# A two-block network on one core: the first block's projections multiply the raw input, and the tokens' norm factors follow on the products

## The chip, the core and the metric

The kernel runs on one core of one Trainium2 chip, in one launch. The metric is the device time of an execution in microseconds (us), lower is better. Before the change three executions took 1520.32, 1525.59 and 1520.54 us, with a median of 1520.54. The profile comes from a further execution.

## What is computed

256 tokens of width 1024 pass through two network blocks. The first block starts with an RMS norm and one wide projection of the normalised tokens, whose columns feed a recurrent mixer (RWKV), a sparse attention (its queries, keys, values and an index of keys) and two gates:

```
def rmsnorm(x, g):
    xf = x.astype(jnp.float32)
    y = xf * lax.rsqrt(jnp.mean(xf * xf, axis=-1, keepdims=True) + NORM_EPS)
    return (y * g.astype(jnp.float32)).astype(x.dtype)
...
        u = rmsnorm(h, norm1_g)
        proj = u @ w_in
...
        p_rwkv, p_att, p_idx, p_gate = jnp.split(proj, c, axis=-1)
        y_a = rwkv7_mix(token_shift(p_rwkv, tshift_mu), ...)
...
        q, k, v = rope(hv(q)), rope(hv(k)), hv(v)
...
        y_b = dsa_attention(q, k, v, q_idx, k_idx, w_idx)
        g_a, g_b = jnp.split(jax.nn.sigmoid(p_gate), 2, axis=-1)
        merged = g_a * (y_a @ w_o_rwkv) + g_b * (y_b @ w_o_att)
```

A feed-forward layer ends the first block. The second block (a gated delta rule, a dilated attention, then 64 routed experts) takes the larger part of the time and isn't touched by the change.

The norm multiplies all 1024 features of a token by one number, the token's factor rs = 1 / sqrt(mean of squares + eps). A factor per token may stand before the projection or behind it: (rs · x · g) @ w = rs · ((x · g) @ w).

## The kernel before

**Layout.** Activations lie transposed: features on the 128 partitions, tokens along a row. The input `xT` (in the trace `hT`) is 8 feature blocks of 128 x 256. A projection is cut into groups of 256 output columns. The weights of one group are one load of 1 MB (`w`, line 258, issued by SyncE), into two buffers in turn.

**Exact products from short ones.** Each fp32 operand is split in two parts of a shorter float type: a high part (`wh`, a cast on ScalarE, line 272) and the rest (`wl`, a subtraction on VectorE, line 273), in pieces of 128 x 512. The input is split likewise into `uh` and `ul`. `mm3` makes three products of one block: uh·wh, ul·wh, uh·wl. `dense` (line 300) does this for 8 feature blocks and 2 halves of the columns: 48 products of 128 x 256 into one PSUM tile `dps`. All matmuls are recorded at line 286, transposes at 289, so tiles tell them apart.

**The head of the program.** `Rms.pair` (line 373) squares the input (`nsq`, ScalarE), VectorE adds the two blocks of a pair, and TensorE multiplies by a column of ones, which gives the sum of squares of every token (`nps`). `columns` takes the root on ScalarE (line 394) and the reciprocal on VectorE (line 395): `rsc`, one factor per token on the partitions. `rows` spreads it by another product into `rsp`, where the factors lie along a row. `scaled_parts` (line 420) then computes u = x · gain · rs on VectorE (line 426), block by block, and splits it (lines 428 and 429). A `hold` keeps the first weight casts behind the root on ScalarE.

**What follows.** Seven `shift_group` calls (line 459) make the columns of the recurrent mixer: first group 6 (`lor0`), then r, k and v of two halves `g`. Each reads `dps` on ScalarE (line 465) and VectorE (line 466). `rwkv(g)` (line 547) is a long chain over small products. Of its steps these matter here: the VectorE product at line 623 ends `aa`; GpSimd scales it to `bp` and `kp` (lines 628 and 629); TensorE transposes v, `bp` and `kp` (`tps`); and products `mps` follow. `dsa_proj` makes the columns of the attention; `rope` turns them with tables `cos` and `sin`. `gate_steps` makes the gates `ga` and `gb`, four groups each. In `select` VectorE finds the best 64 keys per token (lines 832 to 836), and `attend` makes the softmax `lx`, which TensorE transposes into `xps`.

**What sets the order.** The program is written in the order of the data. A scheduler at build time puts the instructions of all engines into fixed queues by its own estimate of when each can start, so products of later groups fill TensorE between the steps of the chains. On the chip each engine works through its queue in that order.

Of the kernel before, what the change touches and what calls it, by code (L numbers as in the profile page):

```python
# [9 lines left out]
F32 = mybir.dt.float32  # L10
F32R = mybir.dt.float32r
AF = mybir.ActivationFunctionType
ALU = mybir.AluOpType
# [180 lines left out]
def _body(es, tc, A, pat, cat, taps, upto):  # L194
# [45 lines left out]
    more = [None, 0, 0, ""]  # L240
    npart = [0]

    hold = []

    def more_slots(pool_, n, tag="wm"):

        more[:] = [pool_, n, 0, tag]
# [13 lines left out]
    def wsplit(w):  # L261

        out = []
        for o in range(0, w.shape[-1], 1024):
            x = w[:, o:min(o + 1024, w.shape[-1])]
            n = x.shape[-1]
            npart[0] += 1
            hi, lo = (wp.tile([128, 1024], F32R, name="w" + q, tag="w%s%d" % (q, npart[0] % 3), bufs=1) for q in "hl")
            for c in range(0, n, 512):
                e = min(n, c + 512)  # L270
                with tc.issue_after(hold[0]) if hold else nullcontext():
                    nc.scalar.copy(hi[:, c:e], x[:, c:e])  # L272
# [91 lines left out]
    class Rms:  # L364


        def __init__(self, h, ring, gain=None):
            self.h, self.ring, self.gain = h, ring, gain
            self.p = pt("d", "nps")

            nc.scalar.activation(nrm, epsd[:, 0:1], AF.Sqrt)

        def pair(self, g):
            sq = self.ring("nsq")
            nc.scalar.activation(sq, self.h[:, 2 * g:2 * g + 2], AF.Square)
            if self.gain is not None:
                sg = self.ring("nsg")[:, 0, :]
                c = [self.gain[:, 2 * g + b:2 * g + b + 1] for b in range(2)]
                nc.vector.tensor_scalar(sg, sq[:, 0, :], c[0], None, op0=ALU.mult)
                nc.vector.scalar_tensor_tensor(sg, sq[:, 1, :], c[1], sg, op0=ALU.mult, op1=ALU.add)  # L380
                self.sums(2, sg, g)
            nc.vector.tensor_tensor(sq[:, 0, :], sq[:, 0, :], sq[:, 1, :], op=ALU.add)
            self.sums(0, sq[:, 0, :], g)

        def sums(self, o, x, g):

# [30 lines left out]
    def parts():  # L417
        return tuple(ap_.tile([128, NB, S], F32R, name="u" + x, tag="u" + x, bufs=1) for x in "hl")

    def scaled_parts(h, gain, rs, sh=None):  # L420

        hi, lo = parts()
        t = ap_.tile([128, NB, S], F32, name="u", tag="s1", bufs=1)
        for b in range(NB):
            x, xh, xl = t[:, b, :], hi[:, b, :], lo[:, b, :]
            nc.vector.scalar_tensor_tensor(x, h[:, b, :], gain(b), rs, op0=ALU.mult, op1=ALU.mult)
            if sh is None:
                nc.scalar.copy(xh, x)
# [12 lines left out]
    hc = lambda h: slice(64 * h, 64 * (h + 1))  # L441
    r2 = lambda g: lambda name: rp.tile([128, 2, S], F32, name=name, tag="r2%d" % g, bufs=NR2)

    norm = Rms(xT, r2(0))
    for g in range(4):
        norm.pair(g)
    _, uu, _ = scaled_parts(xT, lambda b: pcol("norm1_g", b), norm.rows(norm.columns()))
    hold.append(norm.root.ins)


    omm = rp.tile([128, 14], F32, name="omm")
# [6 lines left out]

    def shift_group(g, dst):
        p = yield from dense(A["w_in"][g], uu)  # L460
        for i in range(2):
            j = 2 * g + i
            q = p[:, 256 * i:256 * (i + 1)]
            d = dst[:, i, :]
            nc.scalar.activation(d, q, AF.Copy, scale=omm[:, j:j + 1])
            nc.vector.scalar_tensor_tensor(d[:, 1:], q[:, 0:S - 1], pcol("tshift_mu", j), d[:, 1:],
                                           op0=ALU.mult, op1=ALU.add)
# [53 lines left out]
                    nc.scalar.copy(part(XT, 1 - side), part(p.rearrange("p (u x) -> p u x", x=128), 1 - side))  # L521

    lor0 = r2(0)("lor0")
    whole(shift_group(6, lor0))
    hold.clear()
    lor = rp.tile([128, 2, S], F32, name="lor")
    sgd = rp.tile([128, S], F32, name="sgd")
    nc.gpsimd.memset(lor[64:128, 0, :], 0.0)
# [242 lines left out]
    def dsa_proj():  # L771

        p = yield from dense(A["w_ix"], uu, m=72)
        xi, xj = d2("xi"), d2("xj")
        nc.gpsimd.memset(xi[64:128, 0, :], 0.0)
        nc.scalar.copy(xi[0:72, 0, :], p[0:72, 0:S])
        for a in range(2):
            nc.sync.dma_start(out=xj[32 * a:32 * a + 32, 0, :], in_=xi[32 * (a ^ 1):32 * (a ^ 1) + 32, 0, :])
        for n in range(2):
            p = pt("d", "wps")  # L780
            mm(p[:, 0:8], xi[:, 0, 128 * n:128 * (n + 1)], cc("widx"), start=True, stop=True)
            nc.scalar.activation(wi[:, n, :], p[:, 0:8], AF.Copy, scale=float(64 ** -0.5 * 8 ** -0.5))
        nc.vector.tensor_tensor(xi[0:64, 1, :], xi[0:64, 0, :], cc("cos", 64), op=ALU.mult)
        nc.vector.tensor_tensor(xj[0:64, 1, :], xj[0:64, 0, :], cc("sin", 64), op=ALU.mult)
        nc.vector.tensor_tensor(ki[0:64, 0, :], xi[0:64, 1, :], xj[0:64, 1, :], op=ALU.add)
        nc.sync.dma_start(out=ki[64:128, 1, :], in_=ki[0:64, 0, :])
        for i in range(2):
            rope((yield from dense(A["w_in"][13 + i], uu)), [(every, qi[:, 2 * i:2 * i + 2])])
        for i in range(2):
            rope((yield from dense(A["w_in"][7 + i], uu)), [(every, qT[:, 2 * i:2 * i + 2])])  # L790
        for i in range(2):
            rope((yield from dense(A["w_in"][9 + i], uu)), [(hf, kz[hf, 2 * i:2 * i + 2, a, :]) for a, hf in enumerate(halves)])
        for i in range(2):
            p = pt("d", "vps")
            for k, (wh, wl) in enumerate(wblocks(A["w_in"][11 + i], 256)):
                for n in range(2):
                    tk = slice(128 * n, 128 * (n + 1))
                    mm3(p[:, 256 * n:256 * (n + 1)], (uu[0][:, k, tk], uu[1][:, k, tk]), (wh, wl), k == 0 and n == 0, k == NB - 1)
                yield
            nc.scalar.copy(vt[:, :, 256 * i:256 * (i + 1)], p.rearrange("p (n c) -> p n c", n=2))  # L800

    ga = ap_.tile([128, NB, S], F32, name="ga", tag="s1", bufs=1)
    gcol = lambda t, g: fl(t[:, 2 * g:2 * g + 2])

    def gate_steps(t, src):

        nc.scalar.activation(t, (yield from dense(src, uu)), AF.Tanh, scale=0.5)

    for g in range(2):
        whole(rkv_proj(g))  # L810
        whole(rwkv(g, yA[:, 2 * g:2 * g + 2]))
    whole(dsa_proj())
    for g in range(4):
        fill.add("ga", gate_steps(gcol(ga, g), A["w_in"][15 + g]))


    bias = dp.tile([128, 2, S], F32, name="bias")
# [84 lines left out]
    for g in range(4):  # L902
        first_term(gcol(ga, g), A["wo_r"][g], ysp, 4)
    for g in range(4):
        gate_group(gcol(gb, g), g, A["w_in"][19 + g])
    tap("ya", fl(yA))
    tap("yb", fl(yB))
    if upto == 2:
# [942 lines left out]
```

## Time and profile before

| | |
|---|---|
| median of three executions | 1520.54 us (1520.32 to 1525.59) |
| the profiled execution | 1519.02 us |
| its span, first to last instruction | 1517.2 us |
| TensorE busy with matmuls | 1439.3 us, 95% of the span |
| VectorE, ScalarE, GpSimd busy | 54%, 39%, 8% |
| HBM read | 357.51 MB, 236 GB/s over the span |

Times in the trace count from the span's start. A row of the timeline gives start, duration, engine, line, operation, output <- inputs with shapes, how many instructions were merged, and in brackets the engine's idle time before it with what ended that. PE is TensorE, PEld its weight load, DVE is VectorE, ACT ScalarE, POOL GpSimd and SP SyncE. The matmuls overlap in their pipeline, so what one costs is the distance from its start to the next one's start, not its duration. [...]

### The profile page before, as it was taken

What the parts mean: (1) busy time and instruction counts of PE and PEld (TensorE: products, weight loads), DVE (VectorE), ACT (ScalarE), POOL (GpSimd) and SP (SyncE); (2) the same over time, 40 slices, a digit from 0 to 9 for tenths busy, and PEclk for the clock granted to TensorE, in tenths of its full rate; (3) what the DMA queues carried; (4) which work ended last, traced back from release to release, by engine and by line L of the source; (5) the groups of instructions that cost most, each with busy time, mean ns of one, the idle gap of its engine ahead of it and who ended that gap; (6) DMA issues with size and microseconds to landing.
All of it is one profiled execution on the core that took longest, in us unless ns stands there. A gap on an engine that the chain in (4) does not pass through costs nothing. (4 is left out here: it accounts for less than half of the span.)

```text
span 1517.2 us, 28014 instructions
## 1 busy us (share of the span) xinstructions
PE 1439.3 (95%) x11310; PEld 1155.6 (76%) x11310; DVE 816.5 (54%) x1673; ACT 588.2 (39%) x1208; POOL 119.5 (8%) x120
## 2 busy tenths in 40 slices
PE   6999999989999979899999999999999999988997
PEld 6788998989999969798898999997554544543543
DVE  4787498568888867845854677653122111211211
ACT  5543256545444457434624555552111111111110
POOL 2143210000000000310230000100000000000000
PEclk9999999989999989899999999999999999999999
DMA  5311144649977345221321433875999999999996
GB/s 197 125 47 44 65 160 140 222 144 423 402 292 294 114 151 189 84 84 60 136 84 56 168 111 112 335 286 198 355 407 422 422 422 422 421 422 422 421 423 263
DMA packets 58627, 362.10 MB, mean 239 GB/s; under 512 B 6912, under 2 KB 7552, under 8 KB 20352
## 3 DMA queue, kind: packets, MB, share of 16 engines
q1 hardware_dynamic: 56912, 357.77, 60.6%
q10 hardware_dynamic: 1584, 2.52, 0.5%
q8 instruction: 90, 1.47, 0.4%
q14 instruction: 41, 0.34, 0.1%
HBM read 357.51 MB, written 1.05 MB: 236 GB/s over the span
## 5 line engine op out<-in xcount | busy, mean ns | idle before, releaser
L286 PE MATMUL dps<-uh,wh 128*128 128x256 f32 x1280 | 375.9, 294 | 4.1 <-ACT wh L272 2.1
L286 PE MATMUL dps<-uh,wl 128*128 128x256 f32 x1280 | 364.9, 285 | 4.0 <-DVE wl L273 4.0
L286 PE MATMUL dps<-ul,wh 128*128 128x256 f32 x1280 | 365.6, 286 | 0.1
L286 PEld LDWEIGHTS dps<-uh,wh 128*128 128x128 f32 x1280 | 244.7, 191 | 14.8 <-issue 8.6
L286 PEld LDWEIGHTS dps<-uh,wl 128*128 128x128 f32 x1280 | 244.3, 191 | 6.3 <-DVE wl L273 4.8
L286 PEld LDWEIGHTS dps<-ul,wh 128*128 128x128 f32 x1280 | 244.4, 191 | 5.8 <-issue 4.3
L273 DVE TENSOR_TENSOR wl<-w,wh 128x512 fp32r<-128x512 f32 x267 | 192.3, 743 | 59.4 <-ACT wh L272 58.0
L286 PE MATMUL gup<-wx,xg 128*32 128x512 f32 (+2 forms) x1016 | 205.0, 615 | 17.7 <-DMA wx<-in_w_exp_dram 17.6
L272 ACT CAST wh<-w 128x512 fp32r<-128x512 f32 x267 | 154.3, 615 | 143.0 <-PE dps L286 97.2
L272 ACT CAST wh<-wm 128x512 fp32r<-128x512 f32 x200 | 116.2, 618 | 128.8 <-PE dps L286 84.3
L286 PEld LDWEIGHTS gup<-wx,xg 128*32 128x32 f32 (+2 forms) x1016 | 58.5, 123 | 140.9 <-issue 106.8
L273 DVE TENSOR_TENSOR wl<-wm,wh 128x512 fp32r<-128x512 f32 x200 | 138.2, 721 | 50.6 <-ACT wh L272 48.8
L1695 DVE TENSOR_TENSOR yl<-dnp,yh 128x512 fp32r<-128x512 f32 x54 | 37.3, 691 | 154.5 <-ACT yh L1694 154.5
L1669 DVE COPY cs<-pxt 128x1 f32<-128x1 f32 x27 | 4.3, 158 | 215.2 <-PE pxt L289 215.2
L286 PE MATMUL dnp<-wx,hT 128*32 128x512 f32 (+1 forms) x528 | 101.5, 597 | 2.4 <-DMA wx<-in_w_exp_dram 1.7
L1675 ACT ACTIVATE sgx<-gup 128x256 f32<-128x256 f32 x27 | 10.4, 385 | 221.3 <-PE gup L286 221.3
L1694 ACT CAST yh<-dnp 128x512 fp32r<-128x512 f32 x54 | 31.7, 587 | 120.6 <-PE dnp L286 120.6
L286 PEld LDWEIGHTS dnp<-wx,hT 128*32 128x32 f32 (+1 forms) x528 | 28.0, 120 | 49.5 <-issue 41.3
L286 PE MATMUL acc<-PT,yh 128*128 128x256 f32 x216 | 55.1, 293 | 0.0
L286 PE MATMUL gat<-P,hth 128*128 128x256 f32 (+1 forms) x224 | 54.7, 287 | 0.0
L286 PE MATMUL acc<-PT,yl 128*128 128x256 f32 x216 | 53.0, 283 | 0.6 <-DVE yl L1695 0.6
L971 DVE SCALAR_TENSOR_TENSOR ada<-wm,ct,ada 128x512 f32<-128x512 f32 x76 | 53.2, 745 | 0.0
(530 smaller groups left out, 2786.9 us busy)
## 6 DMA issues: line engine op xcount, KB each, us to landing
wx<-in_w_exp_dram SPq DMA_DIRECT2D x159, 1024.0 KB, 16.0
w<-in_w_in_dram SPq DMA_DIRECT2D x44, 1024.0 KB, 4.9
wm<-in_w_ada_dram SPq DMA_DIRECT2D x22, 1024.0 KB, 8.6
wm<-in_w_in_dram SPq DMA_DIRECT2D x21, 1024.0 KB, 4.9
wh<-in_w_exp_dram SPq DMA_DIRECT2D x33, 512.0 KB, 15.9
wl<-in_w_exp_dram SPq DMA_DIRECT2D x33, 512.0 KB, 14.7
wm<-in_ffn_in_dram SPq DMA_DIRECT2D x16, 1024.0 KB, 10.4
wm<-in_ffn_out_dram SPq DMA_DIRECT2D x7, 1024.0 KB, 10.0
```

The source lines that it names most:

```text
L272: nc.scalar.copy(hi[:, c:e], x[:, c:e])
L273: nc.vector.tensor_sub(lo[:, c:e], x[:, c:e], hi[:, c:e].bitcast(F32))
L286: latest[0] = nc.tensor.matmul(*args, **kw)
L971: nc.vector.scalar_tensor_tensor(y, x, ct[:, k:k + 1], y, op0=ALU.mult, op1=ALU.add)
L1669: nc.vector.tensor_copy(self.cs, px[:, 256:257])
L1675: nc.scalar.activation(sg, self.pg[:, 0:256], AF.Silu)
L1694: nc.scalar.copy(yh[:, quar(c, 512)], pd)
L1695: nc.vector.tensor_tensor(yl[:, quar(c, 512)], pd, yh[:, quar(c, 512)].bitcast(F32), op=ALU.subtract)
```

## The change

The input is split right after it has landed: `raw_pair` casts x · gain on ScalarE and takes the rest on VectorE, without rs. The squares are still made first, but their sums (`finish`), the root, the reciprocal and the spreading come once the first group's 48 products have been written (`factors`). From there the factors are put in behind: `times_rs` multiplies a PSUM tile of 128 x 512 in place on VectorE, for 7 groups of the mixer, 4 of `ga` and 4 of `gb`, 15 in all. For queries and keys the factor goes into the `cos` and `sin` tables once, on GpSimd. For the attention's values and the index weights it is a per-partition scale of ScalarE's copy out of PSUM. The `hold` on the first weight casts is gone.

```
@@ Rms @@
-            self.sums(0, sq[:, 0, :], g)
+            if self.later is None:
+                self.sums(0, sq[:, 0, :], g)
+            else:
+                self.later.append((sq[:, 0, :], g))
+
+        def finish(self):
+            self.p = pt("d", "nps")
+            for x, g in self.later:
+                self.sums(0, x, g)
...
+    def raw_pair(u, h, gain, g):
+        hi, lo = u
+        for b in (2 * g, 2 * g + 1):
+            nc.scalar.activation(hi[:, b, :], h[:, b, :], AF.Copy, scale=gain(b))
+            nc.vector.scalar_tensor_tensor(lo[:, b, :], h[:, b, :], gain(b), hi[:, b, :].bitcast(F32), op0=ALU.mult, op1=ALU.subtract)
...
-    norm = Rms(xT, r2(0))
+    norm = Rms(xT, r2(0), None, [])
+    uu = parts()
     for g in range(4):
         norm.pair(g)
-    _, uu, _ = scaled_parts(xT, lambda b: pcol("norm1_g", b), norm.rows(norm.columns()))
-    hold.append(norm.root.ins)
...
+    def factors():
+        norm.finish()
+        rsc.append(norm.columns())
+        nc.vector.tensor_scalar(rsw, rsc[0], float(64 ** -0.5 * 8 ** -0.5), None, op0=ALU.mult)
+        nc.scalar.copy(rsr, norm.rows(rsc[0]))
+
+    def times_rs(p):
+        p3 = p.rearrange("p (a s) -> p a s", a=2)
+        nc.vector.tensor_tensor(p3, p3, rsr.unsqueeze(1).to_broadcast([128, 2, S]), op=ALU.mult)
+        return p
...
     def shift_group(g, dst):
         p = yield from dense(A["w_in"][g], uu)
+        if not rsc:
+            factors()
+        times_rs(p)
...
-    whole(shift_group(6, lor0))
-    hold.clear()
+    steps = shift_group(6, lor0)
+    for g in range(4):
+        raw_pair(uu, xT, lambda b: pcol("norm1_g", b), g)
+        for _ in range(2 if g else 0):
+            next(steps)
+    whole(steps)
...
                 load_consts(rp, 1)
+                for t in ("cos", "sin"):
+                    nc.gpsimd.tensor_tensor(cc(t), cc(t), rsr, op=ALU.mult)
...
-            nc.scalar.copy(vt[:, :, 256 * i:256 * (i + 1)], p.rearrange("p (n c) -> p n c", n=2))
+            for n in range(2):
+                nc.scalar.activation(vt[:, n, 256 * i:256 * (i + 1)], p[:, 256 * n:256 * (n + 1)], AF.Copy, scale=rsc[0][:, n:n + 1])
...
-    def gate_steps(t, src):
-        nc.scalar.activation(t, (yield from dense(src, uu)), AF.Tanh, scale=0.5)
+    def gate_steps(t, src, first=False):
+        p = yield from dense(src, uu)
+        nc.scalar.activation(t, times_rs(p) if first else p, AF.Tanh, scale=0.5)
```

The scheduler orders the queues anew, which the diff doesn't show. Three places follow, each row an instruction in its queue's order. Line numbers of the changed kernel are its own (283 is its matmul, 286 its transpose, 270 its `wl`, 476 its `times_rs`).

**The head, on TensorE**, before:

```order
L286 MATMUL nps<-ones,nsq 128x1 x8
L286 MATMUL rsp<-cst_74,rsc 128x128 x2
L286 MATMUL dps<-uh,wh 128x256
L286 MATMUL dps<-ul,wh 128x256
L286 MATMUL dps<-uh,wh 128x256
```

and now, where the fifth row is the third of the group's 48 products, the row of "..." stands for the rest of them, and the last row opens the second group:

```order
L283 MATMUL dps<-uh,wh 128x256
L283 MATMUL dps<-ul,wh 128x256
L283 MATMUL nps<-ones,nsq 128x1 x5
L283 MATMUL dps<-uh,wl 128x256
...
L283 MATMUL nps<-ones,nsq 128x1 x3
L283 MATMUL rsp<-cst_74,rsc 128x128 x2
L283 MATMUL dps<-uh,wh 128x256
```

Five of the eight sums stand behind the first two products, three behind the 48th, and the second group waits behind the spreading `rsp`.

**The same head on ScalarE**, now, from the squares to the first reads of the group's result:

```order
L374 ACTIVATE nsq<-hT 128x512 x4
L486 DMA low_107<-in_lowrank_dram 128x512
L486 DMA low_108<-in_lowrank_dram 128x512
L431 ACTIVATE uh<-hT,par 128x256 x4
L269 CAST wh<-w 128x512 x4
L431 ACTIVATE uh<-hT,par 128x256 x4
...
L269 CAST wh<-w 128x512
L401 ACTIVATE rsc<-nps,epsd 128x2
L269 CAST wh<-w 128x512
L471 COPY rsr<-rsp 128x256
L497 ACTIVATE lor_111<-dps,omm 128x256 x2
```

The root (`rsc`), once ahead of every weight cast, now stands behind the first cast of the third group's weights, and both `low` loads are issued ahead of the first `uh`.

**Inside the first `rwkv` chain, on TensorE**, before (`bp` and `kp` are GpSimd's outputs, 30 products of `dps` stand where the row of "..." is):

```order
L286 MATMUL bps<-rk,cst_74 128x256 x2
L289 MATMUL tps<-cst_74,v 128x128 x2
L286 MATMUL dps<-uh,wl 128x256
...
L289 MATMUL tps<-cst_74,bp 128x128
L289 MATMUL tps<-cst_74,kp 128x128
L286 MATMUL dps<-ul,wh 128x256
```

and now:

```order
L283 MATMUL bps<-rk,cst_74 128x256 x2
L286 MATMUL tps<-cst_74,v 128x128 x2
L286 MATMUL tps<-cst_74,bp 128x128
L286 MATMUL tps<-cst_74,kp 128x128
L283 MATMUL dps<-uh,wl 128x256
L286 MATMUL tps<-cst_74,bp 128x128
L283 MATMUL dps<-uh,wh 128x256
L286 MATMUL tps<-cst_74,kp 128x128
L283 MATMUL dps<-ul,wh 128x256
```

The transposes of `bp` and `kp` have moved ahead of those 30 products, which now follow the `mps` products. On VectorE one `wl` that stood between the two products of `aa` went behind them, and a `times_rs` came in ahead of them.

**In `select`, on VectorE**, the queue ahead of the first `lx` that TensorE transposes, before:

```order
L851 TENSOR_SCALAR st<-st 128x2
L273 TENSOR_TENSOR wl<-w,wh 128x512
L835 MAX m_2446<-sc 128x8
L273 TENSOR_TENSOR wl<-w,wh 128x512
L836 MATCH_REPLACE sc<-m_2446,sc 128x256
L854 RECIPROCAL st<-st 128x2
L273 TENSOR_TENSOR wl<-w,wh 128x512
L835 MAX m_2449<-sc 128x8
L855 TENSOR_TENSOR lx<-lx,st 128x2x128
```

and now:

```order
L892 TENSOR_SCALAR st<-st 128x2
L270 TENSOR_TENSOR wl<-w,wh 128x512
L876 MAX m_2452<-sc 128x8
L270 TENSOR_TENSOR wl<-w,wh 128x512
L877 MATCH_REPLACE sc<-m_2452,sc 128x256
L895 RECIPROCAL st<-st 128x2
L476 TENSOR_TENSOR dps<-dps,rsr 128x512
L876 MAX m_2455<-sc 128x8
L896 TENSOR_TENSOR lx<-lx,st 128x2x128
```

A `times_rs` has taken the place of the third `wl`, and another one stands some 20 instructions earlier, among the MAX rows of `select`.

## Rows read from the trace of the kernel before

**Rows 1.** The page, first part: busy us of each engine, share, instructions.

```profile
PE 1439.3 (95%) x11310; PEld 1155.6 (76%) x11310; DVE 816.5 (54%) x1673; ACT 588.2 (39%) x1208; POOL 119.5 (8%) x120
```

**Rows 2.** The timeline of TensorE, head of the program (columns as told above).

```profile
7.86 3.57 PE L286 MATMUL nps<-ones,nsq 128*128 128x1 f32 x16 [7.86 <-DVE nsq L382]
11.98 1.22 PE L286 MATMUL rsp<-cst,rsc 128*128 128x128 f32 x4 [0.55 <-DVE rsc L395]
...
19.50 0.58 PE L286 MATMUL dps<-uh,wl 128*128 128x256 f32 x1 [1.40 <-DVE wl L273]
19.88 0.41 PE L286 MATMUL dps<-uh,wh 128*128 128x256 f32 x1
...
25.00 0.32 PE L286 MATMUL dps<-uh,wh 128*128 128x256 f32 x1
...
27.16 0.28 PE L286 MATMUL dps<-uh,wh 128*128 128x256 f32 x1
```

**Rows 3.** The timeline of VectorE and ScalarE, head of the program.

```profile
7.23 0.28 DVE L452 TENSOR_SCALAR omm<-par 128x14 f32<-128x14 f32 x1 [6.21 <-DMA par<-in_params_dram]
...
11.76 0.17 DVE L395 RECIPROCAL rsc<-rsc 128x2 f32<-128x2 f32 x1 [2.95 <-ACT rsc L394]
...
19.70 3.09 DVE L273 TENSOR_TENSOR wl<-w,wh 128x512 fp32r<-128x512 f32 x5
...
11.47 0.26 ACT L394 ACTIVATE rsc<-nps,epsd 128x2 f32<-128x2 f32 x1 [4.21 <-PE nps L286]
11.47 0.33 ACTq L457 DMA_DIRECT2D low<-in_lowrank_dram  x1
11.85 1.14 ACT L272 CAST wh<-w 128x512 fp32r<-128x512 f32 x2
```

**Rows 4.** The tile w, first 14 us: its two loads and their times to landing.

```profile
L258 SPq DMA_DIRECT2D w<-in_w_in_dram x2: 439/447/455, 2.1 to 2.6; - x2
...
DMA to landing us min/median/max: 7.6/8.9/10.1
```

**Rows 5.** The timeline of TensorE in the first rwkv chain.

```profile
63.34 0.44 PE L289 MATMUL tps<-cst,v 128*128 128x128 f32 x2
66.18 0.58 PE L286 MATMUL dps<-uh,wl 128*128 128x256 f32 x1 [2.40 <-DVE wl L273]
...
71.85 0.27 PE L289 MATMUL tps<-cst,kp 128*128 128x128 f32 x1
```

**Rows 6.** Windows: busy us of PE, PEld, DVE, ACT, POOL; granted clock; DMA share, GB/s.

```profile
64.00:66.00 2.00, 0.00 (x0) 0.00 (x0) 1.97 (x5) 0.55 (x2) 0.00 (x0) 1.00 0.00 0
66.00:68.00 2.00, 1.82 (x8) 1.82 (x9) 2.00 (x4) 0.00 (x0) 1.13 (x2) 0.50 0.41 105
...
216.00:230.00 14.00, 14.00 (x88) 11.25 (x87) 13.54 (x50) 8.21 (x17) 0.00 (x0) 1.00 0.33 107
230.00:240.00 10.00, 8.81 (x72) 8.22 (x72) 10.00 (x35) 6.03 (x16) 0.00 (x0) 1.00 0.29 115
...
310.00:320.00 10.00, 9.18 (x63) 8.99 (x63) 5.75 (x11) 4.36 (x9) 0.00 (x0) 0.83 0.41 145
```

**Rows 7.** The timelines of VectorE and GpSimd beside rows 5.

```profile
65.44 0.69 DVE L273 TENSOR_TENSOR wl<-w,wh 128x512 fp32r<-128x512 f32 x1
66.04 0.69 DVE L623 TENSOR_TENSOR aa<-aa,sg 128x512 f32<-128x512 f32 x1
...
66.87 0.93 POOL L628 TENSOR_TENSOR bp<-aa,PC 128x256 f32<-128x256 f32 x1 [4.48 <-DVE aa L623]
...
69.80 1.06 POOL L629 TENSOR_TENSOR kp<-km,PC 128x256 f32<-128x256 f32 x1
```

**Rows 8.** Line 661, a VectorE product of the added kind that reads PSUM: ns min/median/max.

```profile
L661 DVE TENSOR_TENSOR MB<-mps,cst x4: 682/688/692, 75.2 to 134.1; 128x512 f32<-128x512 f32 x4
```

**Rows 9.** The timeline of TensorE: the wait for lx, and a later wait.

```profile
235.78 0.41 PE L289 MATMUL xps<-cst,lx 128*128 128x128 f32 x2 [1.19 <-DVE lx L855]
...
310.47 0.38 PE L286 MATMUL dps<-mgh,wh 128*128 128x256 f32 x1 [1.43 <-ACT mgh L897]
```

More of the change, by code (lines that the diff above doesn't have):

```diff
@@ L241, in _body @@
     npart = [0]
-    hold = []
     def more_slots(pool_, n, tag="wm"):
@@ L270, in wsplit @@
                 e = min(n, c + 512)
-                with tc.issue_after(hold[0]) if hold else nullcontext():
-                    nc.scalar.copy(hi[:, c:e], x[:, c:e])
+                nc.scalar.copy(hi[:, c:e], x[:, c:e])
                 nc.vector.tensor_sub(lo[:, c:e], x[:, c:e], hi[:, c:e].bitcast(F32))
@@ L364, in _body, with __init__ @@
     class Rms:
-        def __init__(self, h, ring, gain=None):
-            self.h, self.ring, self.gain = h, ring, gain
-            self.p = pt("d", "nps")
+        def __init__(self, h, ring, gain=None, later=None):
+            self.h, self.ring, self.gain, self.later = h, ring, gain, later
+            if later is None:
+                self.p = pt("d", "nps")
             nc.scalar.activation(nrm, epsd[:, 0:1], AF.Sqrt)
@@ L382, in pair @@
             nc.vector.tensor_tensor(sq[:, 0, :], sq[:, 0, :], sq[:, 1, :], op=ALU.add)
-            self.sums(0, sq[:, 0, :], g)
+            if self.later is None:
[3 more added lines that the diff above has]
+        def finish(self):
+            self.p = pt("d", "nps")
+            for x, g in self.later:
+                self.sums(0, x, g)
         def sums(self, o, x, g):
@@ L442, in _body @@
     r2 = lambda g: lambda name: rp.tile([128, 2, S], F32, name=name, tag="r2%d" % g, bufs=NR2)
-    norm = Rms(xT, r2(0))
+    norm = Rms(xT, r2(0), None, [])
+    uu = parts()
     for g in range(4):
         norm.pair(g)
-    _, uu, _ = scaled_parts(xT, lambda b: pcol("norm1_g", b), norm.rows(norm.columns()))
-    hold.append(norm.root.ins)
+    rsr = rp.tile([128, S], F32, name="rsr")
+    rsw = rp.tile([128, 2], F32, name="rsw")
+    rsc = []
+    def factors():
[7 more added lines that the diff above has]
+        return p
     omm = rp.tile([128, 14], F32, name="omm")
@@ L781, in dsa_proj @@
             mm(p[:, 0:8], xi[:, 0, 128 * n:128 * (n + 1)], cc("widx"), start=True, stop=True)
-            nc.scalar.activation(wi[:, n, :], p[:, 0:8], AF.Copy, scale=float(64 ** -0.5 * 8 ** -0.5))
+            nc.scalar.activation(wi[:, n, :], p[:, 0:8], AF.Copy, scale=rsw[:, n:n + 1])
         nc.vector.tensor_tensor(xi[0:64, 1, :], xi[0:64, 0, :], cc("cos", 64), op=ALU.mult)
@@ L813, in _body @@
     for g in range(4):
-        fill.add("ga", gate_steps(gcol(ga, g), A["w_in"][15 + g]))
+        fill.add("ga", gate_steps(gcol(ga, g), A["w_in"][15 + g], True))
     bias = dp.tile([128, 2, S], F32, name="bias")
@@ L904, in _body @@
     for g in range(4):
-        gate_group(gcol(gb, g), g, A["w_in"][19 + g])
+        whole(gate_steps(gcol(gb, g), A["w_in"][19 + g], True))
     tap("ya", fl(yA))
```

## The prediction

> **What bounds the kernel now.** I read the page's first part to find the engine, then the timelines of the head, where the change acts, then the places downstream where VectorE gets new work. TensorE is busy for 1439.3 of 1517.2 us [rows 1], 95%. So a microsecond counts if TensorE idles in it or runs slowly. The largest stop is at the start. TensorE makes the sums from 7.86 to 11.43, spreads the factors from 11.98, makes a few products, and still stops for `wl` before 19.50 [rows 2]. Only from there do products follow without a gap. [...] From 25.00 to 27.16 they are 18 steps of 0.12 us, which is the upper level. By 27.16 the first group's 48 products are all but done (two products of the second group have slipped between). I take 27.16 as the moment from which the second group runs.
>
> After the head, TensorE's rows hardly stop until 63.8. There it waits 2.40 us for a `wl` [rows 5]. The window behind that stop has a granted clock of 0.50, so an idle stretch of 2.4 us cost the upper level too [rows 6]. VectorE is busy for 1.97 of 2 us in the stop: it is late, not waiting. The next place of that kind is `select`, where VectorE is busy for 10.00 of 10 us, and TensorE waits 1.19 us for `lx` [rows 6, 9].
>
> **The head.** Removed: eight gain products (line 426), and the wait of the first casts for sums, root and spreading. What then ends last is the weights. The parameters are there at 7.23 [rows 3], so the raw split of the first four blocks runs while the load of `w` is still on its way. That load is issued at 2.15 and lands 7.6 us later [rows 4], at 9.75. The second `low` load, issued at 11.47 [rows 3], now goes out about 5 us earlier and competes, so I take 10.0. One cast of `wh` (0.6, half of the pair at 11.85) gives the first product at 10.6. Behind two products stand five sums, 10 of the 16 records that took 3.57 us [rows 2]: 2.2 us, so the remaining 46 products start at 13.2. The first `wl` is there at 11.3 and later ones follow every 0.60 (five in 3.09 [rows 3]), each good for 12 products, so nothing else stops them.
>
> How many of them run slowly, no row of this start shows. If as many as now, some 25, they end at 13.2 + 25 × 0.213 + 21 × 0.12 = 21.0. Five sums and two products already occupy TensorE ahead of them, so it may be half as many: 13.2 + 13 × 0.213 + 33 × 0.12 = 19.9. I take the middle, 20.5, and both ends for the range.
>
> Then comes a new wait. TensorE makes three sums (0.7 to 1.3), and its queue stands behind the spreading: root 0.26, reciprocal 0.17, and the four records of `rsp`, 1.22 us at the lower level, about 0.6 at the upper [rows 2, 3]. In ScalarE's queue a weight cast stands ahead of the root, but it starts when the 48th product ends and lasts 0.6, no longer than the sums. So about 1.9 us pass, and the second group starts at 22.4 instead of 27.16: **4.8 us gained**, with ends at 4.0 and 6.0.
>
> **The transposes in the first chain.** This is the cost that the diff doesn't show. Up to the last product of `aa`, VectorE gets one `times_rs` (0.60 back to back) and loses one `wl` that moves behind (0.60), so relative to TensorE's work `aa` ends where it did, near 66.7, and GpSimd delivers the last `kp` at 69.80 + 1.06 = 70.9 [rows 7]. Today TensorE fills that time with 30 products, and meets the last of these transposes at 71.85 [rows 5]. Now the transposes stand first in its queue, so it must stop from 63.8 until `bp` at 67.8, and again until 70.9, with a few products between. It then leaves this place 0.95 us sooner, but with 30 products undone: 30 × 0.12 − 0.95 = **2.6 us lost**. Nothing behind takes that up: the same products are left, in later gaps that other products fill today. If the clock stays at the lower level for as long again after 70.9, another 1.5 us goes (about 15 products at 0.213 instead of 0.12). The ends are 0 and 5.
>
> **The other multiplications.** The added kind, 128 x 512 from PSUM, takes 0.688 us in the row of line 661 [rows 8], like the cast's remainder from SBUF (0.69 [rows 7]), and 0.60 back to back. So 15 cost 9.0 us of VectorE, which is busy for 54% of the span [rows 1]. They lie on the path only where VectorE is full. In `select` two come ahead of `lx` and one `wl` goes behind: **0.6 us lost** on the wait at 235.78, with ends at 0 and 3. The upper end is both multiplications, 1.2 us, and then a fall of the clock as behind a wait of 1.43 us at 310.47 [rows 9]: the granted clock of that 10 us window is 0.83 [rows 6], so about 1.7 us went.
>
> [...]
>
> Two GpSimd products for `cos` and `sin` run in a stretch where GpSimd is idle, and the tables are wanted by `rope` more than 50 us later. They would cost 2 us only if a chain stood behind them. The two scaled copies for each half of `vt` add four small ScalarE instructions, under 0.5 us each, and ScalarE is busy 39% of the span [rows 1]. The load queue's order stays the same in the head. The experts' loads later are started by work that comes earlier by the same amount.
>
> **Sum.** 4.8 − 2.6 − 0.6 = 1.6 us against the profiled execution's 1519.02: 1517.4. The median of the runs shown is 1.5 us higher, by the same sum 1518.9. I forecast **1518.0 us**, between them. A measurement of this kernel can tell about 0.5%, 7.6 us, from no change, so this would read as no change.
>
> **Rivals.**
>
> *The head's gain passes whole* (chance 0.25). If VectorE's chain comes early enough that TensorE finds `bp` ready, the second term is 0, and with the third near 0 the time is 1519.0 − 4.8 = 1514.2, with the best head 1513. For it: all engines start sooner. Against it: VectorE is busy without a gap up to `aa` [rows 6, 7], and starts from TensorE's results.
>
> *VectorE becomes the bound* (0.15). This is the slower side. Eleven of the 15 multiplications fall into stretches where VectorE is full: seven in the mixer's groups and four in `select` and `attend`. If each holds up TensorE by its 0.60, that is 6.6 us, and with 2.6 for the transposes it is 9.2 against 4.8 gained: 1519.0 + 4.4 = 1523.4. It decides once more than about eight come ahead of something that TensorE waits for at that moment. Against it: in 216 to 230 us TensorE is busy throughout while VectorE is at 13.54 of 14 [rows 6].
>
> *The change doesn't start the work sooner* (0.15). If the clock stays low for all of the first group, since TensorE is fed with gaps, the 46 products end at 13.2 + 46 × 0.213 = 23.0, sums and spreading at the lower level take 3.0, and the second group starts at 26.0. Then 1.2 us is gained and 3.2 lost: 1521.0.
>
> **How the numbers follow.** The forecast has 0.45 and a range of its own of 1515 to 1521. The range 1512 to 1524 takes in the rival of the whole gain with the best head and a microsecond below it, and most of the slower one. Faster by over 0.5% means below 1512.9: the tail of the first rival, 0.09. Slower by over 0.5% means above 1528.1: the slower rival with every upper bound, 0.04. The rest, 0.87, is no change that a measurement can tell.
>
> **What would show it.** In the changed profile the first product of `dps` should begin near 10.6, the second group near 22.4, with an idle stretch of about 1 us ahead of `rsp`. In the first chain TensorE should wait for GpSimd's `bp` in place of `wl`, some 4 us, then again for `kp`, and the granted clock should fall there as now. Ahead of the first `xps` the wait should be near 1.8. The forecast is wrong if the second group starts before 21 or after 24, if the waits for `bp` are missing, or if new waits on VectorE of more than 2 us appear between 80 and 300 us.

## The result and the profile after

| | before | after |
|---|---|---|
| median of 16 runs each, same chips | 1521.62 us | 1531.74 us |
| ratio after / before, 95% interval | | 1.0062 [1.0050, 1.0073] |
| the profiled execution, its span | 1519.02, 1517.2 us | 1524.81, 1523.0 us |

The change makes the kernel slower by 10 us, where 1518.0 with a range to 1524.0 was forecast. The profiled execution lies at the fast end: 3 of 16 runs took 1524.8 to 1524.9 us at a mean granted clock of 0.981 or 0.982 (a share of TensorE's full clock), the others 1529 to 1533 at 0.976 to 0.979.

TensorE is as full as before [rows 1], and busy for 2.7 us longer on the same 11310 instructions:

```profile
PE 1442.0 (95%) x11310; PEld 1163.7 (76%) x11310; DVE 819.1 (54%) x1681; ACT 589.9 (39%) x1211; POOL 123.0 (8%) x122
```

The head came out as hoped. The timeline of TensorE, to be held against [rows 2]:

```profile
9.72 0.58 PE L283 MATMUL dps<-uh,wh 128*128 128x256 f32 x1 [9.72 <-ACT wh L269]
...
10.31 2.13 PE L283 MATMUL nps<-ones,nsq 128*128 128x1 f32 x10
12.30 0.56 PE L283 MATMUL dps<-uh,wl 128*128 128x256 f32 x1
...
15.43 0.32 PE L283 MATMUL dps<-ul,wh 128*128 128x256 f32 x1
...
19.31 0.72 PE L283 MATMUL nps<-ones,nsq 128*128 128x1 f32 x6
20.86 0.71 PE L283 MATMUL rsp<-cst,rsc 128*128 128x128 f32 x4 [0.83 <-DVE rsc L402]
21.33 0.36 PE L283 MATMUL dps<-uh,wh 128*128 128x256 f32 x1
```

The second group starts at 21.33 instead of 27.16. This is the earliest of all: in the profiles of the eleven runs below that have this head it starts between 21.88 and 23.87. Then the first chain, TensorE and below it GpSimd and VectorE, to be held against [rows 5, 7]:

```profile
56.99 0.44 PE L286 MATMUL tps<-cst,v 128*128 128x128 f32 x2
61.30 0.48 PE L286 MATMUL tps<-cst,bp 128*128 128x128 f32 x1 [3.87 <-POOL bp L667]
62.31 0.47 PE L286 MATMUL tps<-cst,kp 128*128 128x128 f32 x1 [0.54 <-POOL kp L668]
...
67.17 1.08 PE L283 MATMUL mps<-zr,aa 128*64 128x256 f32 x8
```

```profile
59.49 0.68 DVE L662 TENSOR_TENSOR aa<-aa,sg 128x512 f32<-128x512 f32 x1
...
60.31 0.93 POOL L667 TENSOR_TENSOR bp<-aa,PC 128x256 f32<-128x256 f32 x1 [4.37 <-DVE aa L662]
...
63.24 1.06 POOL L668 TENSOR_TENSOR kp<-km,PC 128x256 f32<-128x256 f32 x1
```

TensorE stops ahead of the transposes, as foreseen, and still reaches `mps` 6.85 us earlier than before (67.17 against 74.02). But the 30 products are not done, and the second chain's first products (`lps`) stand behind them in the queue, and behind 80 small products of the first chain (`sps`) that came after `lps` before. The rows of before, and of after, in which the second chain begins:

```profile
87.30 1.02 PE L286 MATMUL lps<-lor,low 128*128 128x512 f32 x2
```

```profile
92.32 1.02 PE L283 MATMUL lps<-lor,low 128*128 128x512 f32 x2
...
125.72 0.33 PE L286 MATMUL tps<-cst,bp 128*128 128x128 f32 x1 [2.73 <-POOL bp L667]
```

The first chain is 6.3 us early and the second 5.0 us late: it starts 11 us later relative to the first. So the two overlap less, and TensorE stops a second time, for the second chain's `bp`, which before stood behind other work. The last products of the mixer, before and after:

```profile
188.38 0.28 PE L286 MATMUL yps<-SAz,MB 128*64 128x64 f32 x2
```

```profile
188.84 0.28 PE L283 MATMUL yps<-SAz,MB 128*64 128x64 f32 x2
```

By the mixer's end the head's 5.8 us are gone. The rest comes in stages that the change didn't edit. The windows of the feed-forward layer, before and after (TensorE is busy throughout in both, and the count in brackets is its number of products):

```profile
360.00:400.00 40.00, 40.00 (x355) 40.00 (x354) 37.63 (x61) 19.13 (x34) 0.00 (x0) 1.00 1.01 422
...
440.00:520.00 80.00, 80.00 (x682) 80.00 (x681) 69.66 (x112) 37.62 (x67) 0.00 (x0) 1.00 0.59 225
```

```profile
360.00:400.00 40.00, 40.00 (x338) 40.00 (x337) 35.69 (x57) 18.20 (x33) 0.00 (x0) 1.00 1.01 421
...
440.00:520.00 80.00, 80.00 (x673) 80.00 (x672) 68.68 (x110) 37.15 (x66) 0.00 (x0) 1.00 0.63 239
```

At the same granted clock of 1.00 a product takes 40 / 355 = 0.113 us and 80 / 682 = 0.117 us before, 0.118 and 0.119 us after. The products of this layer are the same, in the same order.

### The profile page after: what moved, and what is told of

It reads as the page before. It is cut to its first block, busy times and chain, and to the rows that moved or that the text cites. A ratio compares the mean times of both kernels' runs of the same rounds, so it can differ in the third digit from the quotient of the medians.

```text
span 1523.0 us, 28039 instructions
## 1 busy us (share of the span) xinstructions
PE 1442.0 (95%) x11310; PEld 1163.7 (76%) x11310; DVE 819.1 (54%) x1681; ACT 589.9 (39%) x1211; POOL 123.0 (8%) x122
## 4 chain that ended last, share of the span: by engine, by line
PE 66%; DMA 23%; DVE 5%; ACT 2%; POOL 2%; issue 1%; SPq 0%; DVEq 0%; ACTq 0%; POOLq 0%
PE dps L283 35%; DMA wx<-in_w_exp_dram 15%; PE acc L283 5%; PE sps L283 5%; DMA wh<-in_w_exp_dram 5%; PE gup L283 4%; DMA wl<-in_w_exp_dram 3%; PE vdp L283 2%; PE dnp L283 1%; PE sps L286 1%; PE gat L283 1%; PE sgu L283 1%; DVE wl L270 1%; PE ksp L283 1%; PE vps L283 1%
## 5 line engine op out<-in xcount | busy, mean ns | idle before, releaser
L283 PE MATMUL gup<-wx,xg 128*32 128x512 f32 (+2 forms) x1016 | 200.8, 600 | 19.5 <-DMA wx<-in_w_exp_dram 19.5
L283 PE MATMUL gat<-P,htl 128*128 128x256 f32 (+1 forms) x224 | 54.4, 282 | 0.0
```

Source lines behind the costliest of these rows:

```text
L283: latest[0] = nc.tensor.matmul(*args, **kw)
```

## The experiments

Three theories were to be told apart. **O** (order): the transposes moved ahead of 30 products hold the second chain back. **M** (multiplications): the 15 products on VectorE hold TensorE up. **P** (pace): something makes each 128x256 product slower. In the table the difference is that of the medians of a run and of the kernel before on the same chip, and the products are those of the window 440 to 520 us. The intervals are some 0.3% wide, so a difference of less than about 2 us is not told from none.

| run | median, us | difference | ratio [95%] | products |
|---|---|---|---|---|
| before_again | 1520.42 | −1.1 | 1.0001 [0.9987, 1.0014] | 682 |
| after_again | 1531.64 | +10.2 | 1.0071 [1.0053, 1.0089] | 673 |
| held | 1525.39 | +3.9 | 1.0024 [1.0009, 1.0040] | 672 |
| held_nomul | 1520.99 | −0.5 | 1.0001 [0.9989, 1.0013] | |
| before_down64 | 1525.62 | +4.4 | 1.0032 [1.0018, 1.0047] | 672 |
| after_up64 | 1525.69 | +4.5 | 1.0027 [1.0011, 1.0044] | 682 |
| held_up64 | 1519.00 | −2.2 | 0.9987 [0.9968, 1.0005] | 682 |
| held_up64_nomul | 1515.32 | −5.6 | 0.9965 [0.9948, 0.9982] | |
| held_pad512 | 1524.68 | +3.5 | 1.0034 [1.0018, 1.0051] | 673 |
| held_pad128 | 1520.39 | −0.6 | 1.0003 [0.9986, 1.0020] | 685 |
| held_pad192 | 1512.76 | −8.2 | 0.9949 [0.9934, 0.9964] | 693 |
| held_up64_pool | 1523.16 | +2.2 | 1.0015 [0.9999, 1.0031] | |
| down64_w64 | 1530.93 | +8.3 | 1.0056 [1.0041, 1.0072] | 672 |
| held_192all | 1513.16 | −9.5 | 0.9943 [0.9925, 0.9961] | 702 |
| before_192all | 1513.76 | −8.9 | 0.9946 [0.9931, 0.9961] | 708 |

### Both kernels once more

> The kernel before itself, as a control for the time and for TensorE's pace. In the first profile of it the 128x256 products followed each other by 0.113 us (360 to 400 us) or 0.118 us (400 to 530 us), in the profile of the changed kernel by 0.118 to 0.120 us in the same, unchanged stage, which is 4.2 of the 5.8 us by which the two spans differ. Theory P (the pace belongs to the program): again 0.113 to 0.118 us and no 0.120 in 360 to 530 us. Rival (the pace belongs to the single execution or chip): another mixture, 0.120 among it. Time: ratio 1.000 within 0.001 by either.

> The changed kernel itself. Theory P: 0.118 to 0.120 us again from 360 to 530 us, and the time is 1.005 to 1.007 of the kernel before. Rival: if the pace belongs to the execution, the profile can show 0.113 too, and the span then comes some 4 us nearer to the kernel before on the same chip. The waits in the mixer (6.9 us for bp in 3 waits, the second chain's first lps near 92.7 us) are the same by all theories.

The pace belongs to the program: 682 and 673 again in 440 to 520 us. The stretch of 0.113 us did not: in 360 to 400 us the second profile of the kernel before has 0.118 us. The profile of after_again is of a longer execution (1533.1 us), and its windows show a part of what the shorter one was spared. 120 to 140 us, of after and of after_again:

```profile
120.00:130.00 10.00, 7.13 (x100) 6.21 (x101) 4.33 (x10) 3.85 (x11) 5.59 (x4) 1.00 0.34 113
130.00:140.00 10.00, 8.84 (x71) 6.29 (x69) 9.25 (x17) 2.60 (x8) 4.36 (x3) 1.00 0.01 2
```

```profile
120.00:130.00 10.00, 7.27 (x87) 6.18 (x87) 5.15 (x12) 4.37 (x12) 5.59 (x4) 0.82 0.31 102
130.00:140.00 10.00, 9.60 (x71) 6.85 (x72) 5.38 (x11) 2.51 (x7) 1.60 (x2) 0.84 0.03 11
```

Behind the second chain's stop for `bp` (6.9 us for `bp` in three waits in both) the granted clock falls, and the mixer's last `yps` comes at 192.74 instead of 188.84; 1.4 us of that is a later head. The profile of after_up64 (below), with the same queues, shows the fall too (0.78 and 0.88 in the same windows): it came in two of three profiled executions. The other 4.3 of the 8.2 us between the two spans of the changed kernel arise behind the mixer, and their cause stays open.

### The order put back: held

```
-    for g in range(2):
-        whole(rkv_proj(g))
-        whole(rwkv(g, yA[:, 2 * g:2 * g + 2]))
+    whole(rkv_proj(0))
+    first, second = rwkv(0, yA[:, 0:2]), rkv_proj(1)
+    for _ in range(8):
+        next(first)
+    for _ in range(20):
+        next(second)
+    held[0] = latest[0].ins
+    whole(first)
...
+                with tc.issue_after(held[0]) if g == 0 and dst is not VT else nullcontext():
                     for j in range(2):
                         tr(p[:, 128 * j:128 * (j + 1)], src[:, j, tk], ident)
```

> The changed kernel with TensorE's order in the first rwkv chain put back: the transposes of bp and kp are held behind 32 products of the next groups, as they stood before the change. Theory O (order): the head's 6.5 us was spent because the second chain waits for products that had moved behind the first chain's transposes. So the waits for bp go below 1.5 us in all, the second chain's first lps comes near 81.5 us instead of 92.7, the mixer ends some 6 us earlier than in the changed kernel, and the time is 5 to 6 us below it, about 0.999 to 1.002 of the kernel before. Rival M (the 15 multiplications on VectorE hold TensorE up): the chains start sooner but end where they did, and the ratio stays at 1.004 to 1.007.

The waits of TensorE from 40 to 200 us in after, and in held:

```profile
PE tps L286 <- POOL bp L667: 6.9, 3, 3.9
PE tps L286 <- POOL kp L668: 0.9, 2, 0.5
PE zps L286 <- DVE Y L765: 0.8, 1, 0.8
```

```profile
PE dps L283 <- DVE wl L270: 3.4, 1, 3.4
PE tps L286 <- POOL bp L669: 2.2, 1, 2.2
```

The first chain's stop is one for `wl` again, as before the change [rows 5], 1 us longer. The second chain starts at 86.03, not 81.5: this execution's head was 2.6 us early, not 6.5. The mixer's last `yps` comes at 189.17, no earlier than in after (188.84) and 3.6 us earlier than in after_again. Counted from the first transposes of `v`, which leaves the head out, the mixer takes 125.0 us before, 128.3 in held, 131.9 in after and 134.4 in after_again. The time fell by 6.2 us: theory O holds for the time, with 3.6 to 6.1 us of it in the mixer. The stop of 2.2 us for the second chain's `bp` was not expected: waits below 1.5 us were.

### Without the multiplications: held_nomul, held_up64_nomul

```
     def times_rs(p):
         p3 = p.rearrange("p (a s) -> p a s", a=2)
-        nc.vector.tensor_tensor(p3, p3, rsr.unsqueeze(1).to_broadcast([128, 2, S]), op=ALU.mult)
         return p
```

> As held, but without the 15 multiplications of the products by the norm factors in PSUM, so the mixer's columns and the gates lack their factor. Rival M: 6 to 9 us faster than held. Theory O: within 2 us of held (0.6 us of it in the select stage), since VectorE has room at most places.

> Both repairs, and without the 15 multiplications in PSUM (the mixer's columns and the gates lack their factor). If the three costs (order 6.2 us, address some 6 us, multiplications 4.4 us) are separate and the head's gain is what is left, this is 4 to 5 us faster than held_up64, 0.995 to 0.997 of the kernel before. Rival: with the address repaired TensorE is faster and VectorE's work weighs more, or the multiplications were hidden there: outside 3 to 6 us.

They cost 4.4 us beside held and 3.5 us beside held_up64 (its edit is below): less than rival M's 6 to 9, more than theory O's 2 and the 0.6 us of the prediction. TensorE waits in two places of the mixer. Its waits from 40 to 200 us in held_up64, and in held_up64_nomul:

```profile
PE dps L283 <- DVE wl L270: 3.4, 1, 3.4
PE tps L286 <- POOL bp L671: 2.2, 1, 2.2
```

```profile
PE dps L283 <- DVE wl L270: 2.4, 1, 2.4
```

The first chain's stop is 1.0 us longer with them, and the second chain's stop is there only with them. VectorE, GpSimd and TensorE at that stop in held_up64:

```profile
112.46 0.68 DVE L666 TENSOR_TENSOR aa<-aa,sg 128x512 f32<-128x512 f32 x1
...
115.46 1.88 DVE L270 TENSOR_TENSOR wl<-w,wh 128x512 fp32r<-128x512 f32 x3
...
115.01 2.80 POOL L671 TENSOR_TENSOR bp<-aa,PC 128x256 f32<-128x256 f32 x1
...
117.86 0.33 PE L286 MATMUL tps<-cst,bp 128*128 128x128 f32 x1 [2.15 <-POOL bp L671]
```

and in held_up64_nomul:

```profile
108.93 0.68 DVE L665 TENSOR_TENSOR aa<-aa,sg 128x512 f32<-128x512 f32 x1
...
111.73 0.61 POOL L670 TENSOR_TENSOR bp<-aa,PC 128x256 f32<-128x256 f32 x1
```

With them `aa` ends 3.5 us later, 2.1 us of it since the second chain started that much later (83.95 against 81.89). The second `bp` then runs beside three `wl` and takes 2.80 instead of 0.61 us, and TensorE waits. Without them there is no stop.

The two built programs differ in more than the 15 instructions. Without the multiplications the scheduler also gives TensorE the queue of the kernel before through the rest of the mixer, product by product; with them, in held_up64, products and transposes of the second chain stand in another order. So 3.5 us is the price of the multiplications together with the order that comes with them. No run took out the one and kept the other.

### The place of the input's parts: before_down64, after_up64, held_up64, held_pad512

`uh` and `ul` are the moving operands of most products. In the kernel before they were allocated behind the two small tiles `rsc`; the change calls `parts()` first, and so `rsc` comes behind. Every other tile of these products kept its place. Tiles of the second block that use the same place later (`hth`, `mgh`) moved with them, so in this way the change does touch that block. The starts in bytes per partition, from the built programs:

```
          uh      ul      wh (three buffers)     uh behind a multiple of 1024
before    54336   62528   13312, 21504, 37888    64
after     54272   62464   13312, 21504, 37888     0
```

before_down64 allocates `uh` and `ul` first in the kernel before (and asks for the same two places once more ahead of the feed-forward layer, which adds no instruction), after_up64 and held_up64 allocate `rsc` first in the changed kernel and in held, and held_pad512 leaves 512 bytes free:

```
     norm = Rms(xT, r2(0))
+    made = parts()
...
-    _, uu, _ = scaled_parts(xT, lambda b: pcol("norm1_g", b), norm.rows(norm.columns()))
+    _, uu, _ = scaled_parts(xT, lambda b: pcol("norm1_g", b), norm.rows(norm.columns()), None, made)
```

```
     norm = Rms(xT, r2(0), None, [])
+    norm.made = ap_.tile([128, 2], F32, name="rsc", tag="rsc", bufs=2)
     uu = parts()
```

```
+    ap_.tile([128, 128], F32, name="pad", tag="pad", bufs=1)
     uu = parts()
```

> The kernel before with one allocation moved: the two halves of the split input, uh and ul, are allocated ahead of the two 32-byte tiles rsc, as the change does by the way. They then lie 64 bytes lower in each partition (54272 and 62464 instead of 54336 and 62528); every queue keeps its order. Theory A (address): the 128x256 products of uh and ul then follow each other by 0.119 to 0.120 us in place of 0.118, from the first block to 1010 us, and the time is 1.003 to 1.005 of the kernel before (some 3840 products by 0.0015 to 0.002 us). Rival S (something else of the changed program slows the products): 0.118 us and 1.000.

> The changed kernel with rsc allocated ahead of uh and ul, so that these lie where they lay before the change. Queues keep the changed kernel's order. Theory A: products by 0.118 us again, 5 to 7 us faster than the changed kernel, 1.002 to 1.003 of the kernel before. Rival S: as the changed kernel, 1.006 to 1.007.

> Both repairs: TensorE's order in the first chain put back (held) and rsc allocated ahead of uh and ul. Theories O and A together: 0.118 us, the waits as in held, 5 to 7 us faster than held's 1.0024 and so 0.998 to 0.999 of the kernel before, which is the gain of the head less what VectorE's multiplications cost (4.4 us between held and held_nomul). Rival S: as held, 1.002.

> held with 512 bytes left free ahead of uh and ul, so that they begin 512 bytes behind a multiple of 1024, where the weights' parts begin. Theory A with the address within 1024 bytes as what counts: a pace that is neither that of offset 0 (0.119 to 0.120) nor that of 64 (0.118), perhaps down to 0.113, the fastest that any stretch has shown; the time between 0.985 (all at 0.113) and 1.003 of the kernel before. If only whether the start is a multiple of 128 bytes counts, 0.119 to 0.120 and 1.002 as held. Rival S: as held.

One execution of the changed kernel already shows both paces. Products of `acth`, the feed-forward layer's other operand, which the change didn't move, and right behind them products of `uh`:

```profile
361.86 0.28 PE L283 MATMUL acc<-acth,wh 128*128 128x256 f32 x1
...
363.75 0.28 PE L283 MATMUL acc<-actl,wh 128*128 128x256 f32 x1
...
364.94 0.28 PE L283 MATMUL dps<-uh,wl 128*128 128x256 f32 x1
...
365.90 0.28 PE L283 MATMUL dps<-ul,wh 128*128 128x256 f32 x1
```

The first two rows are 16 products apart, 0.118 us each, the last two 8 products, 0.120 us each. The window 440 to 520 us in before_down64 and in after_up64:

```profile
440.00:520.00 80.00, 80.00 (x672) 80.00 (x671) 68.64 (x111) 37.16 (x66) 0.00 (x0) 1.00 0.63 239
```

```profile
440.00:520.00 80.00, 80.00 (x682) 80.00 (x681) 70.16 (x113) 37.42 (x67) 0.00 (x0) 1.00 0.66 253
```

Theory P has its cause (A in the expectations, for address), and the first three came out inside the expected numbers: 64 bytes in the place of an operand, with every queue in its old order, slow the products of the kernel before to the pace of the changed one and speed up those of the changed one. The place isn't all: in the stretch of 0.113 us of the first profile the products of `uh` and of `acth` ran at 0.113 alike, in their usual places. A distance of 512 is as bad as 0. With both repairs the kernel is 2.2 us below the kernel before, which the interval does not tell from no change.

### Whose place, and better ones: held_pad128, held_pad192, down64_w64, held_192all, before_192all

The edits are pads as above, of 128 and 192 bytes in held. down64_w64 leaves 64 bytes free ahead of the weights' tiles in before_down64 (`uh` and `ul` are asked for once), so that `uh` is where it was before the change and `wh` has followed. The last two put 192 bytes ahead of `uh` in held and in the kernel before, and ahead of the feed-forward layer's tiles, whose `acth` held_pad192 had shifted to 512.

> held with uh and ul 128 bytes behind a multiple of 1024. Starts of 0 and 512 gave 0.119 to 0.120 us, starts of 64 gave 0.118 and in some stretches 0.113. If the pace depends on the start within 128 bytes: 0.119 to 0.120 and 1.002 to 1.003 of the kernel before. If within 256 or 512 bytes: another pace, 0.113 if a larger distance helps more, then 0.99.

> held with uh and ul 192 bytes behind a multiple of 1024. If the start within 128 bytes counts, this is as a start of 64: 0.118 us and 0.998 to 0.999 of the kernel before. If a larger distance to the weights' start helps more: 0.113 to 0.117 and 0.99 to 0.997.

> before_down64 with 64 bytes left free ahead of the weights' tiles too, so that uh, ul, wh and wl all begin 64 bytes behind a multiple of 1024: uh lies at 54336 again, its place in the kernel before, and the weights have followed it. Theory D (the distance between the moving operand's place and the weights' place counts): the distance is 0 as in before_down64, so 0.119 to 0.120 us and 1.003 of the kernel before. Rival B (uh's own place counts): 0.118 us and 1.000.

> held with uh and ul 192 bytes behind a multiple of 512, and the feed-forward layer's acth and actl, which held_pad192 left at 0 and whose products ran at 0.120 us there, at 192 too. Theory A: their 528 products come to 0.113 to 0.118 us, 1 to 3 us below held_pad192, 0.993 to 0.995 of the kernel before. Rival (the pace of these products has another reason): as held_pad192, 0.995.

> The kernel before with the same places for uh, ul, acth and actl as held_192all. If the address alone makes the gain, most of it comes without the change: some 5 to 7 us below the kernel before, 0.995 to 0.997, and held_192all lies about 2 us below this, as held_up64 lay below the kernel before. Rival: the gain of held_pad192 came from the change's earlier start: 1.000.

The window once more, in down64_w64 and in held_192all:

```profile
440.00:520.00 80.00, 80.00 (x672) 80.00 (x671) 68.87 (x110) 37.14 (x66) 0.00 (x0) 1.00 0.62 238
```

```profile
440.00:520.00 80.00, 80.00 (x702) 79.15 (x701) 69.91 (x117) 37.87 (x68) 0.00 (x0) 1.00 0.62 236
```

With `uh` at its old place and the weights moved after it the pace is the slow one, 672 products: the distance counts, not the operand's own place. (Its pad moves all later tiles by 64 bytes as well. Why its time is 3.8 us above before_down64, mostly behind 600 us, stays open.)

The windows mix products of two operands. Taken apart, the mean distance from one product to the next from 360 to 530 us is, by the operand's distance behind a multiple of 1024 from the weights' start (runs without a stretch of 0.113 us at 64 and 320):

| distance, bytes | `uh`, `ul`, us | `acth`, `actl`, us |
|---|---|---|
| 0 | 0.120 | |
| 64 | 0.118 | |
| 128 | 0.119 | |
| 192 | 0.113 | |
| 320 | | 0.118 |
| 448 | | 0.114 |
| 512 | 0.120 | 0.120 |
| 704 | | 0.113 |
| 832 | | 0.118 |

A distance of 128 is not like 0, and 192 is not like 64: the rule "the start within 128 bytes" fell. The pairs 64 and 320, 192 and 704, 0 and 512 look alike, as if the distance within 256 bytes counted; no run was made to test that. 192 is the best of the five tried for `uh`. held_192all did not beat held_pad192 in the medians, although the products of `acth` came from 0.120 to 0.113 us; the intervals overlap.

The two last runs settle what is whose. before_192all is 8.9 us below the kernel before, where 5 to 7 were expected. At a good place the kernel before takes 1513.8 us and the changed one with its order repaired 1513.2: the two beat the kernel before by 0.5% and can't be told from each other. The expected 2 us between them did not show. The gain is the place's.

### The gates' factor on GpSimd: held_up64_pool

```
+        if first == "pool":
+            t3 = t.rearrange("p (a s) -> p a s", a=2)
+            nc.scalar.copy(t, p)
+            nc.gpsimd.tensor_tensor(t3, t3, rsr.unsqueeze(1).to_broadcast([128, 2, S]), op=ALU.mult)
+            nc.scalar.activation(t, t, AF.Tanh, scale=0.5)
+            return
```

> held_up64 with the factor of the four ga gates moved off VectorE: ScalarE copies the product into the gate's place, GpSimd multiplies it there, ScalarE takes the tanh. VectorE loses four multiplications of 0.6 us in the select and attend stages, where it is full. If these hold TensorE up there: 1 to 2 us faster than held_up64. Rival: the multiplications that cost stand in the mixer's chains, ahead of what the chains wait for, and nothing is gained here: within 0.5 us of held_up64.

A miss for both sides: 4 us slower than held_up64 in the medians, with intervals that just overlap. The profiled executions are equally long (1518.6 and 1519.0 us). The waits from 230 to 260 us in held_up64, and in held_up64_pool:

```profile
PE xps L286 <- DVE lx L908: 1.1, 1, 1.1
```

```profile
PE xps L286 <- DVE lx L914: 2.0, 1, 2.0
PE ops L283 <- ACT xt L920: 1.1, 1, 1.1
```

The scheduler ordered `attend` anew: transposes moved ahead of products, and TensorE waits for `xt` as well, 2.0 us more in all in this stretch. Whether the multiplications there cost anything by themselves stays open.

## Why the prediction was wrong

Each part of the change, from the differences in the table:

| part | forecast | measured | from |
|---|---|---|---|
| the earlier start, net of all else | −4.8 | −5.6 | held_up64_nomul |
| the multiplications, with the order that comes with them | +0.6 | +3.5 | held_up64 less held_up64_nomul |
| the order of the transposes | +2.6 | +6.7 | after_up64 less held_up64 |
| the place of `uh` and `ul` | none | +5.7 | after_again less after_up64 |
| sum | −1.6 | +10.2 | after_again |

The parts add up to the sum by the way they are taken, so the sum confirms nothing. Other pairs of runs give 4.4 us for the multiplications (held less held_nomul), 6.2 for the order (after_again less held), and 4.4 and 6.1 for the place (before_down64, and held less held_up64).

**The head** was right, step by step. First product at 9.72 (10.6 forecast), 14 slow products behind the five sums (13 to 25), an idle 0.83 us ahead of `rsp` (about 1), the second group at 21.33 (22.4), a gain of 5.8 us, inside the ends of 4.0 and 6.0. Over all twelve profiles with this head the second group starts at 22.6 on the average, a gain of 4.6 us (4.8 forecast). Its 0.213 and 0.12 us for a product are the paces of before, 24 products from 19.88 to 25.00 us and 18 from 25.00 to 27.16 [rows 2]; in after 13 go at 0.213 us from 12.66 to 15.43. That the slow ones here are a lower level of the clock, as the forecast takes them and the spreading, no run shows: the granted clock is 1.00 from 7 to 30 us in both profiles. The same 0.213 us stands beside a granted clock of 0.50 in the first chain of before (66.99 to 69.33 us). Why the head's first products are slow stays open.

**The transposes** were right in kind and in place, too small in size. The wait for `bp` is 3.87 us (4 forecast), the granted clock falls there (0.67 in 60 to 70 us, 0.83 before), and `aa` ends where it did: 3.2 us behind the transposes of `v`, 3.4 before. The step that failed is "30 × 0.12 − 0.95 = 2.6 us lost", which prices the undone products as work to be caught up. What it left out is who waits for that work. The second chain, which ends last, stands behind those products, and its own `bp` became a second stop, behind which the clock fell in two of three profiles. TensorE's waits from 40 to 200 us are 3.0 us before, 5.9 in held and 9.3 in after; with the fall of the clock behind the second stop the order costs 6.1 us in the mixer (after_again less held), without it 3.6 (after less held). The range's upper end of 5 was too low as well.

**The multiplications** were sought in the wrong place. "In `select` two come ahead of `lx`": there the wait for `lx` even shrank, from 1.19 [rows 9] to 0.80 us, where 1.8 was forecast:

```profile
238.63 0.41 PE L286 MATMUL xps<-cst,lx 128*128 128x128 f32 x2 [0.80 <-DVE lx L896]
```

They cost in the mixer, 1.0 us at the first chain's `wl` and 2.2 at the second chain's `bp`. The rival that makes VectorE the bound counted the mixer's groups, at twice the price (6.6 us); but it is two stops that cost, not 0.60 us for each multiplication. One `times_rs` takes 0.699 us, beside 0.688 of the row of its kind [rows 8]:

```profile
L476 DVE TENSOR_TENSOR dps<-dps,rsr x15: 677/699/700, 22.0 to 295.3; 128x512 f32<-128x512 f32 x15
```

**The place** was in no term and in no rival. All sums took 0.12 us for a product, before and after, and the allocation that the change turned round counted as nothing, without a reason given. The runs put 4.4 to 6.1 us in its place. The profile of before could have shown that 0.12 us is not the only pace, with 0.113 and 0.117 us in windows of the same clock; that the place sets it, it could not show.

The runs show 0.120 us against 0.113 us by the place alone: `uh` and `ul` at a distance of 0 in held, of 192 in held_192all. Why the distance counts, no run here shows.

The forecast's own warning sign, new waits on VectorE of over 2 us between 80 and 300 us, did not appear by name. It came as a wait on GpSimd (2.73 us for `bp`), one step behind VectorE. No sign that it named looked at the pace of the products.

## What to carry to other kernels

Before pricing a reordered queue, follow the displaced work to the chain that ends last: look for the stops and the fall of the clock that it brings there, beside its own duration. A change that adds, drops or swaps an allocation can move operands of matmuls that it never touches, so compare the tiles' places in the two programs, and the products' count in a full window of an unchanged stage. Try a few pads ahead of the moving operand: here 192 bytes gave 8.9 us in the kernel before, and the change with both repairs 2.2, which is not told from nothing.

## What was not expected of the hardware

- The pace of a stream of 128x256 products at a granted clock of 1.00 is not one figure: 0.113 to 0.120 us. In the feed-forward layer it goes by the distance of the moving operand's start from a multiple of 1024, where the weights start: 0 and 512 gave 0.120, 128 gave 0.119, 64 (and 320, `acth` in the kernel before) gave 0.118 with stretches of 0.113, 192 gave 0.113.
- At a distance of 64 the same program ran the same stretch (360 to 400 us) at 0.113 us in one execution (before) and at 0.118 us in another (before_again). What decides that stays open.
- A stop of TensorE of 2.73 us left the granted clock at 1.00 in one execution of the changed kernel (after, 120 to 140 us). In another (after_again), with the same 6.9 us of waits for `bp` in all, 0.82 and 0.84 followed.
- A GpSimd product of 128x256 took 0.61 us with VectorE idle (held_up64, from 113.64 us) and 2.80 us beside three VectorE subtractions (held_up64, from 115.01 us); beside five of them in the changed kernel's first chain it took 0.93 to 1.06 us (after, 60.31 to 64.30 us), and the five took 4.76 us, where five at the head of before took 3.09 [rows 3]. What decides which of the two engines is held up stays open.
